# Row halves of the matrix array in a two-block network's recurrence: both heads of a pair side by side

## Chip, core and metric

The kernel runs on one core of one Trainium2 chip. The metric is the device time of one execution in microseconds (us); less is better. Five engines work beside each other: TensorE (PE in the profile, its weight loads PEld), VectorE (DVE), ScalarE (ACT), GpSimd (POOL), and SyncE (SP), which here issues nearly all transfers.

## What is computed

The reference runs two network blocks on a sequence of 1024 tokens. The first (windowed attention, a gated recurrence, a convolution and experts, two layers) is not touched by the change. The second block normalises its input, projects it with one wide matrix, and runs two branches: a gated unit that mixes blocks of 128 tokens (`gmlp`), and a recurrence with 16 heads of 64 channels:

```python
def wkv7_scan(r, w, k, v, kk, a):
    # S_t = S_{t-1} diag(w_t) + (S_{t-1} (-kk_t)) (kk_t * a_t)^T + v_t k_t^T ;  o_t = S_t r_t
    def step(state, inp):
        r_t, w_t, k_t, v_t, kk_t, a_t = inp
        sa = jnp.einsum('bhvk,bhk->bhv', state, -kk_t)
        state = (state * w_t[:, :, None, :]
                 + sa[..., None] * (kk_t * a_t)[:, :, None, :]
                 + v_t[..., None] * k_t[:, :, None, :])
        o_t = jnp.einsum('bhvk,bhk->bhv', state, r_t)
        return state, o_t
```

Both branches are then projected, gated, added and normalised. All of it is float32.

## The kernel before

The kernel doesn't step token by token. It cuts the sequence into 16 chunks of 64 tokens. Inside a chunk the dependence of each token on the earlier ones is a triangular 64x64 system for each head, which is inverted ahead of time; from chunk to chunk only the 64x64 state of each head is carried. Two heads make a pair: head p of a pair (p is 0 or 1) has its 64 channels on partitions 64p to 64p+63, and there are 8 pairs (q).

Four stages of the second block matter here.

- **Preparation of the pairs** (`rw_prepare`, `rw_pair`, lines 1525 to 1709). While TensorE computes the projection of r, k and v for pair q+1 (`gemm_feat`, whose matrix products are lines 168 to 170), the scaled vectors of pair q are formed. `s3` writes two tensors: `AR` (for each chunk alpha, the scaled -kk, and r) and `BK` (for each chunk beta and k; on the second head's rows in the other order, so that head p's beta lies at index p). `s4` forms the triangular matrices: beta times alpha for each head and chunk (line 1677), 16 products of which each reads all 128 partitions. For this the alphas lie in a tensor `raz` (`self.az`), set to zero once (line 1535), with head p's alphas copied to its own rows by ScalarE (line 1661); the zeros take the other head out of the sum. `s4` masks the result to `LT` and stores it.
- **Inverses** (`rw_inverses`, lines 1711 to 1764). The 64x64 triangular matrices are cut into 32x32 blocks. For four groups of pairs (b, two pairs each) the diagonal blocks are inverted by elementwise steps on GpSimd (the last group on VectorE), stored, and loaded again in another layout, and in four units of one pair and half a sequence the off-diagonal block follows by two products: `Lo` times the first block's inverse (line 1753) gives `Y`, and `Y` times the second block's inverse (line 1760) gives the block of `XT`, which is stored for the recurrence. Head p's blocks lie on partition quarters: the first product reads rows 64p to 64p+31 and writes partitions 64p+32 to 64p+63, the second the other way. Each head's 8 products are followed by its copy out of PSUM (`evac`, lines 123 and 125, in turn on ScalarE and VectorE).
- **The value path of the gated unit** (`gmlp_v`): a projection in 32 tiles.
- **The recurrence** (`rw_scan`, lines 1767 to 1897), in the background of the gated unit's and the gates' projections. For each chunk, two calls of `prepare` for the next chunk form all products of `BK` with `AR` of both heads (line 1796): each reads the 64 rows of one head, has 128 columns of weights and 128 columns of data. VectorE masks the result to `RL` and `MR`. The first call takes head 0, the second head 1; in each, two groups of four pairs, one PSUM bank after the other. The chunk's other products are lines 1836, 1849, 1870 and 1890; in line 1890 the second kind (`SV` with `AR`) uses 64x64 tiles, head p reading rows 64p and writing partitions 64p of one bank.

Background work is written as generators: after each tile of a projection, `tick` advances every generator of `self.bg` by one step (to its next `yield`). `drain` advances them with no projection between. A compiler pass orders each engine's instructions by this program order and by its own estimate of when they are ready, adds the semaphores, and gives each tile's memory free when its last user is done. All stages after the experts run on this one set of queues; each engine works through its queue in order.

```python
def tick(self):
    for _ in range(self.step):
        self.bg = [g for g in self.bg if next(g, self) is not self]
```

A float32 product is recorded as two matrix instructions, each with its weight load. The other names: `pt` are PSUM tiles of one bank (six in these stages), `pg` those of the projections (two).

Of the kernel before, what the change touches and what calls it, by code (L numbers as in the profile page):

```python
# [8 lines left out]
F32 = mybir.dt.float32  # L9
# [10 lines left out]
P = 128  # L20
# [1267 lines left out]
class Block2(Block1):  # L1288
# [236 lines left out]
    def rw_prepare(self, hi, lo, blocks, w, pool):  # L1525
        nc = self.nc
        t = lambda nm, n=512, b=1: pool.tile([P, n], F32, name=nm, tag=nm, bufs=b)
        m0 = t("rm0")
        nc.vector.memset(m0, 1.0)
        nc.vector.memset(m0.rearrange("p (c t) -> p c t", t=64)[:, :, 0:1], 0.0)  # L1530

        wa = pool.tile([P, 2, D], F32R, name="rwa")

        self.az = pool.tile([P, 2, 8, 64], F32, name="raz")
        nc.vector.memset(self.az, 0.0)
        cur = {}

        def mixed(f, t0, acc, out):

            pz, last = t("rpz", 513, 2), cur.get("p")  # L1540
            cur["p"] = pz
            if t0 == 0:
                nc.vector.memset(pz[:, 0:1], 0.0)  # L1543
            else:
                nc.vector.tensor_copy(pz[:, 0:1], last[:, 512:513])
            nc.scalar.copy(pz[:, 1:513], acc)
            if f % 4:
                nc.scalar.activation(out, acc, AF.Copy, scale=self.mu1[:, f:f + 1])
            else:
                nc.vector.tensor_scalar(out=out, in0=acc, scalar1=self.mu1[:, f:f + 1], scalar2=None, op0=ALU.mult)  # L1550
            nc.vector.scalar_tensor_tensor(out=out, in0=pz[:, 0:512], scalar=self.mu[:, f:f + 1], in1=out, op0=ALU.mult, op1=ALU.add)

        def ev_wa(c, t0, tn, acc):
            x = t("mz", 512, 2)
            mixed(0, t0, acc, x)
            self.act(x[0:64], x[0:64], AF.Tanh)
            for j in range(2):
                r, o = slice(64 * j, 64 * j + 64), slice(64 - 64 * j, 128 - 64 * j)
                nc.scalar.copy(wa[r, j, t0:t0 + tn], x[r])
                nc.vector.tensor_tensor(out=wa[o, j, t0:t0 + tn], in0=x[r], in1=f32(wa[r, j, t0:t0 + tn]), op=ALU.subtract)  # L1560

        self.d_Li = [self.tc.dram_tile([P, 32, 32], F32, name=f"dL{g}") for g in range(4)]
        self.d_Xi = [self.tc.dram_tile([P, 2, 32, 32], F32, name=f"dX{g}") for g in range(4)]

        def ev(c, t0, tn, acc):
            f = c // P
            q, kind = divmod(f - 1, 3)
            o = cur["rkv"[kind], t0] = t("m" + "rkv"[kind], 512, 4)
            mixed(f, t0, acc, o)

        def ev_z(c, t0, tn, acc):
            f = c // P
            z, sg = t("mz", 512, 2), t("mzs", 512, 1)
            mixed(f, t0, acc, z)
            self.act(sg, z, AF.Sigmoid)
            nc.gpsimd.tensor_tensor(out=z, in0=z, in1=sg, op=ALU.mult)
            nc.sync.dma_start(out=self.d_z[(f - 25) * P:(f - 24) * P, t0:t0 + tn], in_=z)

        self.gemm_feat(w, 0, P, hi, lo, blocks, ev_wa)
        inv = self.rw_inverses(t)  # L1580
        self.pairs = 0
        pair = iter(())
        for q in range(KT):
            self.bg = [pair, inv]
            self.gemm_feat(w, P + q * 384, 384, hi, lo, blocks, ev)
            for _ in pair:
                pass
            pair = self.rw_pair(q, dict(cur), wa, m0, pool)
        self.bg = [pair, inv]
        self.gemm_feat(w, 25 * P, D, hi, lo, blocks, ev_z)  # L1590

    def rw_pair(self, q, cur, wa, m0, pool):
        nc = self.nc
# [12 lines left out]
        for h in range(2):  # L1606
            e = d[h]
# [40 lines left out]
        def s3(h):  # L1648
            e = d[h]
            r, k, v, a, kk, sq, g, gp, ig, bv = (e[x] for x in ("r", "k", "v", "a", "kk", "sq", "g", "sg", "ig", "n"))  # L1650
            pb = self.pt()
            nc.tensor.matmul(pb, lhsT=self.bones, rhs=sq, start=True, stop=True)
            e["AR"], e["BK"] = AR, BK = t("AR", D), t("BK", D)
            ar = AR.rearrange("p (c x t) -> p c x t", x=2, t=64)
            bk = BK.rearrange("p (c x t) -> p c x t", x=2, t=64)
            V.scalar_tensor_tensor(out=ar[:, :, 0, :], in0=c3(kk), scalar=-1.0, in1=c3(gp), op0=ALU.mult, op1=ALU.mult)
            V.tensor_tensor(out=ar[:, :, 1, :], in0=c3(r), in1=c3(g), op=ALU.mult)
            V.tensor_tensor(out=a, in0=a, in1=kk, op=ALU.mult)
            for p in range(2):
                rows = slice(64 * p, 64 * p + 64)  # L1660
                nc.scalar.copy(self.az[rows, p], ar[rows, :, 0, :])
                V.tensor_tensor(out=bk[rows, :, p, :], in0=c3(a)[rows], in1=c3(ig)[rows], op=ALU.mult)
                V.tensor_tensor(out=bk[rows, :, 1 - p, :], in0=c3(k)[rows], in1=c3(ig)[rows], op=ALU.mult)
            V.tensor_tensor(out=bv, in0=pb, in1=v, op=ALU.mult)
            nc.sync.dma_start(out=self.d_bv[qs, 512 * h:512 * h + 512], in_=bv)
            for src, dst in ((AR, self.d_AR), (BK, self.d_BK)):
                nc.sync.dma_start(out=dst[8 * h:8 * h + 8, :, q, :].rearrange("c p x -> p c x"), in_=src.rearrange("p (c x) -> p c x", c=8))

        def s4(h):
            e = d[h]  # L1670
            bk = e["BK"].rearrange("p (c x t) -> p c x t", x=2, t=64)

            pl, pv = self.pt(), self.pt()
            LT, VT = t("LT"), t("VT")
            for c in range(8):
                for p in range(2):
                    nc.tensor.matmul(pl[64 * p:64 * p + 64, 64 * c:64 * c + 64], lhsT=bk[:, c, p, :], rhs=self.az[:, p, c, :], start=True,
                                     stop=True, skip_group_check=True)
            for i in range(4):
                nc.tensor.transpose(pv[:, P * i:P * i + P], e["v"][:, P * i:P * i + P], self.ident)  # L1680
            V.tensor_tensor(out=c3(LT), in0=c3(pl), in1=self.tri[:, 0, :].unsqueeze(1).to_broadcast([P, 8, 64]), op=ALU.mult)
# [29 lines left out]
    def rw_inverses(self, t):  # L1711
        nc = self.nc
        for b in range(4):
# [20 lines left out]
            for u in range(4):  # L1734
# [3 lines left out]
                for p in range(2):  # L1738
# [7 lines left out]
                    nc.sync.dma_start(out=X1[r1], in_=self.d_Xi[b][n0:n0 + 8, 0].rearrange("n s t -> s n t"))  # L1746
                    nc.sync.dma_start(out=Lo[r1], in_=self.d_LT[q, h, r1, :, 32:64])
                yield
                py = self.pt()
                for p in range(2):  # L1750
                    r1, r2 = slice(64 * p, 64 * p + 32), slice(64 * p + 32, 64 * p + 64)
                    for c in range(8):
                        nc.tensor.matmul(py[r2, 32 * c:32 * c + 32], lhsT=Lo[r1, c, :], rhs=X1[r1, c, :], start=True, stop=True,
                                         tile_position=(64 * p, 64 * p + 32), skip_group_check=True)
                    self.evac(Y[r2].rearrange("p c x -> p (c x)"), py[r2, :256])
                px = self.pt()
                for p in range(2):
                    r1, r2 = slice(64 * p, 64 * p + 32), slice(64 * p + 32, 64 * p + 64)
                    for c in range(8):
                        nc.tensor.matmul(px[r1, 32 * c:32 * c + 32], lhsT=Y[r2, c, :], rhs=XT[r2, c, 32:64], start=True, stop=True,  # L1760
                                         tile_position=(64 * p + 32, 64 * p), skip_group_check=True)
                    self.evac(XT[r1, :, 32:64], px[r1, :256].rearrange("p (c x) -> p c x", c=8))
                nc.sync.dma_start(out=self.d_XT[8 * h:8 * h + 8, :, q, :].rearrange("c p x -> p c x"), in_=XT)
                yield
# [2 lines left out]
    def rw_scan(self, pool):  # L1767
# [18 lines left out]
            nc.sync.dma_start(out=e["XT"], in_=self.d_XT[c])  # L1786
            return e

        def prepare(e, p):

            rows, oth = par[p]
            for g in groups:
                ps = self.pt()
                for q in range(g.start, g.stop):
                    x = (q - g.start) * P
                    nc.tensor.matmul(ps[:, x:x + P], lhsT=e["BK"][rows, q, :], rhs=e["AR"][rows, q, :], start=True, stop=True,  # L1796
                                     skip_group_check=True)
                pv = ps.rearrange("p (q x t) -> p q x t", q=4, x=2)
                V.tensor_tensor(out=e["RL"][p][oth, g, :], in0=pv[oth, :, 0, :], in1=self.tri[oth, 0, :].unsqueeze(1).to_broadcast([64, 4, 64]),
                                op=ALU.mult)  # L1800
# [15 lines left out]
        e = load(0)  # L1816
# [4 lines left out]
        for p in range(2):  # L1821
            rows, oth = par[p]
            V.memset(e["SV"][p][rows], 0.0)
            prepare(e, p)
            yield
        scale(e, 0)
        yield
# [1 line left out]
        for c in range(16):  # L1829
# [8 lines left out]
                for p in range(2):  # L1838
                    (nc.scalar.copy, V.tensor_copy)[p](R[p][par[p][0], g, :], pq(pr)[par[p][0]])
            if n:  # L1840
                prepare(n, 0)
            yield
            for g in groups:
                pu = self.pt()
# [9 lines left out]
            if n:  # L1854

                for p in range(2):
                    rows = par[p][0]
                    nc.gpsimd.tensor_tensor(out=n["SV"][p][rows], in0=e["SV"][p][rows],
                                            in1=self.gc[rows, :, c].unsqueeze(2).to_broadcast([64, KT, 64]), op=ALU.mult)
                prepare(n, 1)  # L1860
                scale(n, c + 1)
            yield
            if n:
# [192 lines left out]
```

## Time and profile before

| | before |
|---|---|
| runs | 4241.87, 4234.22, 4232.11 us (median 4234.22) |
| the profiled execution's own time | 4232.61 us |
| its span, first to last instruction | 4230.7 us |
| mean granted clock of TensorE | 0.961 |
| TensorE busy | 3844.5 us |
| VectorE, ScalarE, GpSimd busy | 2478.8, 1723.2, 1228.8 us |

The profile is of one execution. An engine's busy time is the time in which it had at least one instruction under way; matrix instructions are pipelined, so their own durations overlap and the distance between starts tells the pace. The clock is the share of full speed (2.4 GHz) that TensorE was granted; it has two levels, so 0.5 is 1.2 GHz and a value between is a mean over both. Start times count from the span's start. "x16" is the number of instructions that a row merges, and a bracket at the end of a row is the engine's idle time just before it and what ended it.

### The profile page before, as it was taken

The numbers are of one execution on the slowest core, as the hardware profiler recorded it, in microseconds if no ns is written. First come the engines' busy times: TensorE is split into PE (matmuls) and PEld (weight loads), VectorE is DVE, ScalarE is ACT, GpSimd is POOL, SyncE is SP. The second block draws the span as 40 slices with busy tenths as digits, with TensorE's granted clock in tenths as the row PEclk, the third lists the DMA queues.
The fourth block names the chain that finished last, engine by engine and source line by source line (L and its number), as shares of the span: only waits on it lengthen the run. The fifth ranks groups of instructions, "written<-read, shape, count | busy, mean of one in ns | idle before, by whom it ended". The sixth has DMA issues, their size and how long they took to land. (4 is left out here: it accounts for less than half of the span.)

```text
span 4230.7 us, 71359 instructions
## 1 busy us (share of the span) xinstructions
PE 3844.5 (91%) x28350; PEld 3103.0 (73%) x28350; DVE 2478.8 (59%) x4042; ACT 1723.2 (41%) x2900; POOL 1228.8 (29%) x1036
## 2 busy tenths in 40 slices
PE   7998889896999899888889599898899999999998
PEld 4877787764677688778777487676678888887777
DVE  3067745767677633785675798667776343222533
ACT  3134433622555432443462476554563211122522
POOL 2133233532232223322442222105451122211630
PEclk9999999998999999999999799999999999999999
DMA  7643222164899864332223899544545554444742
GB/s 257 198 123 112 83 70 83 55 217 175 275 305 305 285 209 136 112 97 73 80 91 120 285 367 371 179 126 118 140 126 148 139 135 123 134 136 126 246 129 90
DMA packets 543980, 695.71 MB, mean 164 GB/s; under 512 B 162592, under 2 KB 350368, under 8 KB 536992
## 3 DMA queue, kind: packets, MB, share of 16 engines
q1 hardware_dynamic: 531552, 653.40, 47.8%
q0 software_dynamic: 12096, 37.75, 3.6%
q8 instruction: 224, 3.67, 0.4%
q14 instruction: 108, 0.88, 0.1%
HBM read 530.61 MB, written 160.43 MB: 163 GB/s over the span
## 5 line engine op out<-in xcount | busy, mean ns | idle before, releaser
L154 DVE TENSOR_TENSOR wlo<-raw,whi 128x2048 fp32r<-128x2048 f32 (+2 forms) x320 | 594.6, 1868 | 374.2 <-ACT whi L151 364.2
L151 ACT CAST whi<-raw 128x2048 fp32r<-128x2048 f32 (+2 forms) x354 | 531.8, 1504 | 490.2 <-PE pg L169 200.7
L168 PE MATMUL pg<-hi,whi 128*128 128x512 f32 (+1 forms) x1808 | 719.3, 398 | 2.6 <-DVE cy L450 1.1
L170 PE MATMUL pg<-hi,wlo 128*128 128x512 f32 (+1 forms) x1808 | 698.6, 386 | 0.1
L169 PE MATMUL pg<-lo,whi 128*128 128x512 f32 (+1 forms) x1808 | 698.3, 386 | 0.0
L168 PEld LDWEIGHTS pg<-hi,whi 128*128 128x128 f32 x1808 | 345.9, 191 | 79.2 <-issue 7.1
L169 PEld LDWEIGHTS pg<-lo,whi 128*128 128x128 f32 x1808 | 345.8, 191 | 70.7 <-issue 7.1
L170 PEld LDWEIGHTS pg<-hi,wlo 128*128 128x128 f32 x1808 | 344.9, 191 | 68.0 <-DVE rpz L1543 0.5
L168 PE MATMUL pg<-whi,hi 128*128 128x256 f32 x1200 | 343.4, 286 | 2.2 <-ACT stg L379 2.2
L170 PE MATMUL pg<-whi,lo 128*128 128x256 f32 x1200 | 342.0, 285 | 0.0
L169 PE MATMUL pg<-wlo,hi 128*128 128x256 f32 x1200 | 341.5, 285 | 0.0
L168 PEld LDWEIGHTS pg<-whi,hi 128*128 128x128 f32 x1200 | 229.9, 192 | 13.5 <-issue 5.7
L169 PEld LDWEIGHTS pg<-wlo,hi 128*128 128x128 f32 x1200 | 230.2, 192 | 7.8 <-issue 5.9
L170 PEld LDWEIGHTS pg<-whi,lo 128*128 128x128 f32 x1200 | 229.9, 192 | 7.3 <-issue 6.1
L154 POOL TENSOR_TENSOR wlo<-raw,whi 128x1024 fp32r<-128x1024 f32 (+1 forms) x34 | 97.6, 2874 | 434.9 <-ACT whi L151 434.8
L168 PE MATMUL pg<-whi,xh 128*128 128x512 f32 x512 | 209.6, 409 | 0.0
L169 PE MATMUL pg<-wlo,xh 128*128 128x512 f32 x512 | 204.9, 400 | 1.9 <-DVE wlo L154 1.8
L170 PE MATMUL pg<-whi,xl 128*128 128x512 f32 x512 | 204.6, 400 | 0.8 <-DVE xl L1038 0.8
L1102 POOL DMA_INDIRECT x<-eo,iT x32 | 99.1, 3096 | 249.0 <-DVE eo L1094 235.5
L379 ACT COPY stg<-pg 128x256 f32<-128x256 f32 x118 | 43.8, 371 | 237.8 <-PE pg L170 211.7
L502 PE MATMUL pt<-hZQ,hKS 128*64 128x64 f32 x2592 | 98.0, 229 | 45.8 <-DVE hKS L538 28.6
L1030 POOL DMA_INDIRECT xg<-xn,iT x32 | 56.7, 1772 | 284.8 <-PE pt L1139 267.7
(459 smaller groups left out, 8362.8 us busy)
## 6 DMA issues: line engine op xcount, KB each, us to landing
raw<-in_w_exp_gate_dram SPq DMA_DIRECT2D x64, 1024.0 KB
raw<-in_w_exp_up_dram SPq DMA_DIRECT2D x64, 1024.0 KB
raw<-in_w_exp_down_dram SPq DMA_DIRECT2D x64, 1024.0 KB
raw<-in_k_win_dram SPq DMA_DIRECT2D x124, 512.0 KB
wm<-in_w_mod_dram SPq DMA_DIRECT2D x36, 1024.0 KB
AR<-AR SPq DMA_DIRECT2D x32, 512.0 KB
BK<-BK SPq DMA_DIRECT2D x32, 512.0 KB
mxr<-mix SPq DMA_DIRECT2D x18, 512.0 KB
```

The costliest lines, as they stand in the source:

```text
L151: nc.scalar.copy(hi, r)
L154: i = eng.tensor_tensor(out=lo, in0=r, in1=f32(hi), op=ALU.subtract)
L168: mm(out, lhsT=lh, rhs=rh, start=start, stop=False)
L169: mm(out, lhsT=lh, rhs=rl, start=False, stop=False)
L170: mm(out, lhsT=ll, rhs=rh, start=False, stop=stop)
L379: nc.scalar.copy(s, acc)
L502: nc.tensor.matmul(ps[64 * (c % 2):64 * (c % 2) + 64, c // 2 * 64:c // 2 * 64 + 64], lhsT=KS[:, cc * 64:(cc + 1) * 64], rhs=zq[:, c * 64:( ...
L1030: nc.gpsimd.indirect_dma_start(out=g, out_offset=None, in_=d_h[:, :], in_offset=bass.IndirectOffsetOnAxis(ap=iT[:, e:e + 1], axis=0))
L1102: nc.gpsimd.indirect_dma_start(out=d_x[:, :], out_offset=bass.IndirectOffsetOnAxis(ap=iT[:, e:e + 1], axis=0), in_=o, in_offset=None, comp ...
```

## The change

Three things are changed in the second block, and one `yield` is added.

1. `s4` reads the alphas from `AR` directly: each head's product contracts over its own 64 rows and writes its own 64 partitions. The tensor `raz`, its zeroing and the 32 copies to it are gone.
2. In the inverses, the two heads' products alternate in one group, for the first as for the second product; the copies follow after both heads. Between the copies to `Y` and the second product stands a `yield`, so a unit takes three steps and not two.
3. `prepare` takes a group of four pairs, not a head. It has two PSUM banks, one for each head, and alternates between the heads; the first call takes pairs 0 to 3, the second pairs 4 to 7.

```diff
-        self.az = pool.tile([P, 2, 8, 64], F32, name="raz")
-        nc.vector.memset(self.az, 0.0)
...
-                nc.scalar.copy(self.az[rows, p], ar[rows, :, 0, :])
...
             for c in range(8):
                 for p in range(2):
-                    nc.tensor.matmul(pl[64 * p:64 * p + 64, 64 * c:64 * c + 64], lhsT=bk[:, c, p, :], rhs=self.az[:, p, c, :], start=True,
-                                     stop=True, skip_group_check=True)
+                    rows = slice(64 * p, 64 * p + 64)
+                    nc.tensor.matmul(pl[rows, 64 * c:64 * c + 64], lhsT=bk[rows, c, p, :], rhs=ar[rows, c, 0, :], start=True, stop=True,
+                                     skip_group_check=True)
...
+                halves = [(slice(64 * p, 64 * p + 32), slice(64 * p + 32, 64 * p + 64)) for p in range(2)]
                 py = self.pt()
-                for p in range(2):
-                    r1, r2 = slice(64 * p, 64 * p + 32), slice(64 * p + 32, 64 * p + 64)
-                    for c in range(8):
+                for c in range(8):
+                    for p, (r1, r2) in enumerate(halves):
                         nc.tensor.matmul(py[r2, 32 * c:32 * c + 32], lhsT=Lo[r1, c, :], rhs=X1[r1, c, :], start=True, stop=True,
                                          tile_position=(64 * p, 64 * p + 32), skip_group_check=True)
+                for r1, r2 in halves:
                     self.evac(Y[r2].rearrange("p c x -> p (c x)"), py[r2, :256])
+                yield
                 px = self.pt()
-                for p in range(2):
-                    r1, r2 = slice(64 * p, 64 * p + 32), slice(64 * p + 32, 64 * p + 64)
-                    for c in range(8):
+                for c in range(8):
+                    for p, (r1, r2) in enumerate(halves):
                         nc.tensor.matmul(px[r1, 32 * c:32 * c + 32], lhsT=Y[r2, c, :], rhs=XT[r2, c, 32:64], start=True, stop=True,
                                          tile_position=(64 * p + 32, 64 * p), skip_group_check=True)
+                for r1, r2 in halves:
                     self.evac(XT[r1, :, 32:64], px[r1, :256].rearrange("p (c x) -> p c x", c=8))
...
-        def prepare(e, p):
+        def prepare(e, g):
-            rows, oth = par[p]
-            for g in groups:
-                ps = self.pt()
-                for q in range(g.start, g.stop):
-                    x = (q - g.start) * P
+            pss = [self.pt() for p in range(2)]
+            for q in range(g.start, g.stop):
+                x = (q - g.start) * P
+                for p, ps in enumerate(pss):
+                    rows = par[p][0]
                     nc.tensor.matmul(ps[:, x:x + P], lhsT=e["BK"][rows, q, :], rhs=e["AR"][rows, q, :], start=True, stop=True,
                                      skip_group_check=True)
+            for p, ps in enumerate(pss):
+                oth = par[p][1]
                 pv = ps.rearrange("p (q x t) -> p q x t", q=4, x=2)
...
-            prepare(e, p)
+            prepare(e, groups[p])
...
-                prepare(n, 0)
+                prepare(n, groups[0])
...
-                prepare(n, 1)
+                prepare(n, groups[1])
```

## Rows read from the trace of the kernel before

**Rows 1.** The page's first part: busy us (share of the span) and instructions.

```profile
PE 3844.5 (91%) x28350; PEld 3103.0 (73%) x28350; DVE 2478.8 (59%) x4042; ACT 1723.2 (41%) x2900; POOL 1228.8 (29%) x1036
```

**Rows 2.** Busy time by stretch: us, engines' busy us (instructions), granted clock, DMA share, GB/s.

```profile
2760.00:2920.00 160.00, 150.21 (x792) 116.70 (x790) 117.91 (x174) 89.69 (x155) 55.91 (x69) 0.98 0.38 112
2920.00:3130.00 210.00, 189.15 (x1306) 142.61 (x1307) 157.93 (x233) 99.47 (x180) 101.71 (x132) 0.91 0.50 135
3130.00:3345.00 215.00, 210.16 (x1804) 183.54 (x1803) 112.31 (x245) 95.29 (x182) 23.45 (x16) 1.00 0.49 137
3365.00:3897.00 532.00, 529.47 (x4669) 441.23 (x4670) 180.89 (x334) 108.45 (x202) 121.13 (x85) 1.00 0.46 128
```

**Rows 3.** Single lines on TensorE: instructions, ns min/median/max, first to last start us, form.

```profile
L1796 PE MATMUL pt<-AR,BK x512: 272/272/373, 3364.8 to 3873.5; 64*128 64x128 f32 x171
...
L1753 PE MATMUL pt<-X,Lo x512: 191/191/257, 2925.2 to 3308.3; 32*32 32x32 f32 x171
...
L1760 PE MATMUL pt<-XT,Y x512: 184/191/257, 2928.4 to 3313.3; 32*32 32x32 f32 x171
```

**Rows 4.** Timeline of TensorE, a call of `prepare`: start us, us, what.

```profile
3364.83 2.05 PE L1796 MATMUL pt<-AR,BK 64*128 64x128 f32 x16
3366.81 0.38 PE L1507 MATMUL pt<-gws,gV 128*128 128x128 f32 x1
```

**Rows 5.** Timeline of TensorE, output of a chunk, line 1890.

```profile
3405.94 0.68 PE L1890 MATMUL pt<-AR,SV 64*64 64x64 f32 x16
3406.55 0.69 PE L1890 MATMUL pt<-MR,UV 128*64 128x64 f32 x16
```

**Rows 6.** Timeline of TensorE, line 1677 and what follows it.

```profile
2788.70 1.15 PE L1677 MATMUL pt<-raz,BK 128*64 128x64 f32 x32
2789.78 0.66 PE L1680 MATMUL pt<-k_ident,mv 128*128 128x128 f32 x4
```

**Rows 7.** Timeline of TensorE, one group of the inverses' first product.

```profile
2968.99 0.69 PE L1753 MATMUL pt<-X,Lo 32*32 32x32 f32 x16
2969.61 0.50 PE L169 MATMUL pg<-lo,whi 128*128 128x512 f32 x1
```

**Rows 8.** Timeline of TensorE, where head 1's first product meets head 0's second.

```profile
3205.68 0.59 PE L1753 MATMUL pt<-X,Lo 32*32 32x32 f32 x13
3206.09 0.21 PE L1760 MATMUL pt<-XT,Y 32*32 32x32 f32 x1
...
3206.20 0.57 PE L1760 MATMUL pt<-XT,Y 32*32 32x32 f32 x13
3206.70 0.50 PE L169 MATMUL pg<-lo,whi 128*128 128x512 f32 x1
```

**Rows 9.** TensorE's waits from 2760 to 3365 us: total us, times, longest.

```profile
PE pt L1652 <- DVE rsq L1641: 13.1, 2, 7.9
PE pt L1760 <- issue: 10.3, 4, 4.4
...
PE pt L1760 <- ACT XT L123: 2.1, 2, 1.2
```

**Rows 10.** Timeline of TensorE around one of these waits.

```profile
3119.30 0.91 PE L1677 MATMUL pt<-raz,BK 128*64 128x64 f32 x22
3122.72 0.97 PE L1760 MATMUL pt<-XT,Y 32*32 32x32 f32 x16 [2.51 <-issue]
```

**Rows 11.** Timeline of VectorE at the same place.

```profile
3122.19 0.43 DVE L125 COPY Y<-pt 32x256 f32<-32x256 f32 x1
```

**Rows 12.** Copies to `raz`: instructions, ns min/median/max, first to last start.

```profile
L1661 ACT COPY raz<-AR x32: 603/620/625, 2783.4 to 3174.7; 64x512 f32<-64x512 f32 x32
```

**Rows 13.** The squares of `gmlp_v`, one for each of its 32 tiles.

```profile
L1449 DVE CUSTOM_DVE_ANT_0 mzs<-mz x32: 418/426/1952, 3250.2 to 3346.0; 128x256 f32<-128x256 f32 x32
```

**Rows 14.** Timeline of SP: the load of `gws`.

```profile
3350.21 0.50 SPq L1471 DMA_DIRECT2D gws<-in_k_gws_dram  x1
```

**Rows 15.** Timeline of TensorE: the products that need `gws`.

```profile
3356.28 1.98 PE L1481 MATMUL pt<-gws,gs 128*128 128x512 f32 x4 [2.86 <-DVE gws L1473]
```

More of the change, by code (lines that the diff above doesn't have):

```diff
@@ L1670, in s4 @@
             e = d[h]
-            bk = e["BK"].rearrange("p (c x t) -> p c x t", x=2, t=64)
+            ar, bk = (e[x].rearrange("p (c x t) -> p c x t", x=2, t=64) for x in ("AR", "BK"))
             pl, pv = self.pt(), self.pt()
```

## The prediction

> **What bounds the kernel now.** I read the page's first part for the engines, then the stretches of the last block, then the lines that the diff touches, then TensorE's waits. TensorE is busy 91% of the span, more than any other engine [rows 1]. In the recurrence stretch, 3365 to 3897 us, it is busy 529.5 of 532 us at full clock; VectorE is busy 181 us there, ScalarE 108. What is taken from TensorE there comes off the end. The preparation before it falls into three parts [rows 2]. From 3130 to 3345 us TensorE is again nearly full (210 of 215). From 2920 to 3130 us it is busy 189 of 210 us, VectorE 158, and the mean granted clock is 0.91: no engine is full, TensorE waits for results and then runs slowly. A saving there is worth less than its size.
>
> **What was profiled.** The span is 4230.7 us and the execution's time 4232.6 us, 1.9 us around it. The median of the runs is 4234.2, 1.6 us higher. All sums start from 4232.6.
>
> **The products of a chunk (`prepare`).** Line 1796 has 512 matrix instructions [rows 3]. Each float32 product is recorded as two, and a call makes 16 of them, so there are 32 calls. One call takes from 3364.83 to 3366.81, 1.98 us [rows 4]: 0.12 us for each instruction, all 16 on the same half of the array's rows. The change makes the same 32 calls with the same 16 instructions, but neighbours lie on opposite halves and write different banks. The trace has no 64x128 tiles that alternate between row halves. The nearest rows are 32x32 products of lines 1753 and 1760 where one group runs into the next, on other rows, other columns and another bank [rows 8]. Thirteen alone take 0.41 us, 0.032 each; six alternating singly (the row at 3206.09 and the five left out behind it) take 0.11 us to 3206.20, 0.018 each. So tiles that share neither rows nor columns run side by side at 0.57 of the price. For `prepare` the bounds are no gain (both halves share one path for their weights) and half. A group's fixed part follows from two groups of 64-column tiles: 32 instructions take 1.08 us [rows 6], 16 take 0.61 us [rows 5], so one costs 0.029 and the fixed part is 0.14. A new call is then 0.14 + 8 x (1.98 - 0.14)/16 = 1.06 us, and 32 calls save 32 x 0.92 = 29 us. I take this end, because the alternating rows of [rows 8] come close to a half. The VectorE work behind a call (four products with the mask) is the same in count; it now comes together at the end of a call, while TensorE goes on with the projection. VectorE's 181 of 532 us hide it [rows 2].
>
> **The inverse blocks' products.** Lines 1753 and 1760 have 512 instructions each [rows 3], 64 groups of 16. A group at full clock lasts 2968.99 to 2969.61, 0.62 us [rows 7], of which 16 x 0.032 = 0.50 is work and 0.12 is fixed. Now both heads make one group of 32 alternating instructions: 32 x 0.018 + 0.12 = 0.70 us against 1.24. That is 0.54 us for each of 32 pairs, 17 us of TensorE (bounds: 0, and 20 if the price falls to a half). The trace has 36 of the 64 groups after 3130 us, where TensorE is full, so 9.7 us count there. Of the other 7.6 I count half, 3.8, since TensorE has idle time in that part.
>
> The Trainium skill speaks against this part. Its page "TensorEngine Tiling (Array Packing)", section "Restrictions and Gotchas", says that different row tiles can't access the same PSUM bank at the same time; both heads' products here go to one bank. The trace disagrees where it can be tested: in line 1890 the 64x64 tiles of both row halves write one bank, and their 16 instructions take 3405.94 to 3406.55, 0.61 us, exactly like tiles of all 128 rows in the L1677 group by the fixed part worked out above [rows 5, 6]. By the rule the 17 us would be nothing; by the row they stand.
>
> **The wait between the two products.** Before, the second product stands right behind the first's copy to `Y` in the same step, and TensorE waits: 10.3 us in four places and 2.1 us in two [rows 9]. The view gives "issue" for the four. The one at 3122.72 shows what it was: the copy of `Y` on VectorE started at 3122.19 and took 0.43 us, after other work of that queue [rows 10, 11]. The new `yield` puts a whole projection tile between copy and second product, so these 12.4 us go. I credit 9.6: the 2.6 us after 3130 us in full, and 7 of 9.8 us before, where TensorE may meet the next VectorE result. The waits also lower the clock: from 2920 to 3130 us a mean of 0.91 over 210 us is 19 us of full clock lost [rows 2]. These waits are about 40% of the idle time there, the rest belonging mostly to L1652's 13.1 us [rows 9]; I credit half of that share, 4 us.
>
> **The moved steps.** An inverse group of four units needs 8 + 4 x 2 = 16 steps before and 8 + 4 x 3 = 20 after; the first starts at step 18 of 96 (48 projection tiles of r, k and v, 16 of z, 32 of `gmlp_v`). Groups follow one another, so the last second product moves from step 81 to step 97, one after the last tile of `gmlp_v`. In the trace these products end at 3313 us and `gmlp_v` at 3346 us [rows 3, 13]. What moves with them: the loads of `XT`, `X1` and `Lo` and the store of `XT` on SP's queue, the copies on ScalarE and VectorE. Two places can pay. First, after `gmlp_v` SP loads `gws` at 3350.21 and TensorE already waits 2.86 us for it [rows 14, 15]; the last `XT` store now stands ahead of that load and waits for its copy. `gmlp_v`'s own statistics end at about the same time, so I take 1 us (bounds 0 and 8). The scan's own load of `XT` comes later still. Second, the transfers of the second inverse group now meet another step of a pair; the 7.9 us wait of L1652 is what such a meeting costs at worst [rows 9]. I take 3 us (bounds 0 and 8).
>
> **What is removed or costs nothing.** The 32 copies to `raz`, 0.62 us each [rows 12], leave ScalarE, which is busy 99 of 210 us [rows 2]; I count nothing (up to 3 us of gain through earlier copies). Line 1677's products go from 128-row tiles with zeros to 64x64 tiles on the diagonal. That is the form of line 1890, at the same price [rows 5, 6]: nothing.
>
> **Sum.** 29 + 9.7 + 3.8 + 9.6 + 4 = 56.1 saved, 4 lost, and 1 for loads of the scan that now come a little late: 51 us. 4232.6 - 51 = 4181 us.
>
> **Rivals.**
> A. The row halves share one path for weights, so `prepare` gains nothing: 4181 + 29 = 4210. For it: the alternating rows differ in columns too [rows 8]. Against it: nothing in them hints at a shared path. Chance 0.10.
> B. Two row tiles of one bank take turns in the inverse blocks: 13.5 us less, 4195. This is the time by the Tiling page's rule. Against it stands line 1890 [rows 5]. Chance 0.05.
> C. From 2920 to 3130 us VectorE is the limit and the transfers collide: the 3.8, 7 and 4 us fall away and 5 more are lost, 4201. For it: VectorE's 158 of 210 us [rows 2]. Against it: most of these waits end with one small copy [rows 11]. Chance 0.08.
> D. Slower: each change of row half inside a `prepare` call makes the array empty itself, at the group's fixed 0.14 us. With 512 changes that is 72 us in place of a gain of 29: 4181 + 29 + 72 = 4282. It decides from 22/512 = 0.043 us a change. Against it: neighbours in [rows 8] start 0.01 to 0.03 us apart. The Tiling page's section "Key Properties" has a drain only for a change of mode, not of tile, which the trace's rows bear out. Chance 0.04.
>
> **How the numbers follow.** The forecast has 0.73. Its own range is 4160 to 4200: all bounds in favour (29 + 20 + 12.4 + 8 + 3) give 4160; half of the 14.8 us from 2920 to 3130 gone, and both meeting places at their full 8 us (7 and 5 more), give 4200. To hold 8 in 10 the range takes in B, most of C and half of A: 4160 to 4210. A change within 0.2% (8.5 us) is about what the measurement can't tell from none. A to C are all faster than that. Faster 0.93, same 0.03 (A with C), slower 0.04 (D).
>
> **What would show it.** A `prepare` call of about 1.06 us in the timeline; inverse groups of 32 in about 0.70 us; L1677 still near 1.08; no wait of the second product for `Y`; last inverse product just behind `gmlp_v`; the recurrence stretch about 29 us shorter with TensorE still full. I am wrong if a call stays near 2 us, or if TensorE's waits elsewhere in 2920 to 3130 us grow by what was saved.

## The result, and the profile after

| | before | after |
|---|---|---|
| median of the runs, us | 4234.06 | 4192.65 |
| lowest and highest | 4232.11, 4241.87 | 4187.87, 4195.25 |
| ratio, 95% interval | | 0.990 [0.9888, 0.9913] |
| profiled execution: time, span | 4232.61, 4230.7 | 4195.25, 4193.5 |

The change saves 41.4 us, 1.0%. The forecast was 4181, in a range of 4160 to 4210. Right in direction and range, it promised some 10 us too much.

The two profiles can't be compared by their spans. These are the first transposes of the second block, before and after (instructions, ns min/median/max, first to last start):

```profile
L279 PE MATMUL pt<-dg,x x128: 275/275/582, 2700.5 to 2718.9; 128*128 128x128 f32 x128
```

```profile
L279 PE MATMUL pt<-dg,x x128: 274/275/580, 2710.8 to 2728.8; 128*128 128x128 f32 x128
```

Everything ahead of them is unchanged, and it took 10.3 us longer in the profile after. Over the profiles below this start lies anywhere from 2694.9 to 2710.8 us. So I compare stretches that are cut at the program's own marks: T0, the first L279; T1, the last square of `gmlp_v`; T2, the first product of `prepare`; T3, the last product of the recurrence with `SV`. The marks after, by line:

```profile
L1449 DVE CUSTOM_DVE_ANT_0 mzs<-mz x32: 418/426/1056, 3238.5 to 3334.9; 128x256 f32<-128x256 f32 x32
```

```profile
L1797 PE MATMUL pt<-AR,BK x512: 271/272/374, 3361.0 to 3838.1; 64*128 64x128 f32 x171
```

```profile
L1893 PE MATMUL pt<-AR,SV x512: 217/219/268, 3399.0 to 3866.4; 64*64 64x64 f32 x171
```

Before, T1 and T2 are 3346.0 and 3364.8 [rows 13, 3], and T3 is 3901.9. In us:

| stretch | before | after | difference | forecast |
|---|---|---|---|---|
| T0 to T1, preparation and `gmlp_v` | 645.5 | 624.1 | -21.4 | -24 |
| T1 to T2, the turn to the recurrence | 18.9 | 26.0 | +7.1 | +1 |
| T2 to T3, the recurrence | 537.0 | 505.5 | -31.5 | -28 |
| T3 to the end | 328.9 | 327.0 | -1.9 | 0 |
| T0 to the end | 1530.2 | 1482.6 | -47.6 | -51 |

**The recurrence.** A call of `prepare` after, against 1.98 us in [rows 4] (TensorE's timeline: start us, us, what):

```profile
3360.95 1.16 PE L1797 MATMUL pt<-AR,BK 64*128 64x128 f32 x16
3362.04 1.16 PE L1507 MATMUL pt<-gws,gV 128*128 128x128 f32 x8
```

From start to next start it is 1.09 us; 1.06 were forecast. 32 calls save 28.5 us, and TensorE is still full (stretches: us, engines' busy us in the order of [rows 2], clock):

```profile
3365.00:3862.00 497.00, 496.43 (x4632) 409.18 (x4630) 173.32 (x328) 108.69 (x203) 119.35 (x83) 1.00 0.47 134
```

**The inverses' products.** Against two groups of 0.62 us [rows 7], one of 32:

```profile
2962.05 0.69 PE L1751 MATMUL pt<-X,Lo 32*32 32x32 f32 x32
2962.67 0.50 PE L168 MATMUL pg<-hi,whi 128*128 128x512 f32 x1
```

It takes 0.62 us, as long as half its instructions did. The 32 of a line-1674 group (1677 before) lie on 64x64 tiles now and still take 1.08 us, as in [rows 6]:

```profile
2798.66 1.15 PE L1674 MATMUL pt<-AR,BK 64*64 64x64 f32 x32
2799.74 0.66 PE L1677 MATMUL pt<-k_ident,mv 128*128 128x128 f32 x4
```

**TensorE's waits.** After, from 2760 to 3365 us (total us, times, longest), to be held against [rows 9]:

```profile
PE pt L1759 <- DMA XT<-dX: 11.6, 3, 5.6
PE pt L1649 <- DVE rsq L1638: 9.3, 1, 9.3
PE pt L1634 <- DVE rpz L1542: 6.5, 3, 3.1
PE pt L1674 <- DVE BK L1658: 4.4, 3, 2.7
```

The second product (L1759) hardly waits for `Y` any more (0.3 us). It waits for `XT`'s loads, almost as long in all: 11.6 us against 12.4, of which 5.6 come behind T1. And the sum of TensorE's idle time from T0 to T1 hardly moved; here are the stretches before and after:

```profile
2701.00:3346.00 645.00, 608.68 (x4212) 494.15 (x4212) 420.83 (x714) 315.78 (x577) 183.69 (x220) 0.96 0.44 124
```

```profile
2711.00:3335.00 624.00, 588.69 (x4176) 480.69 (x4176) 422.23 (x709) 290.12 (x541) 189.83 (x220) 0.96 0.45 128
```

Idle is 645.0 - 608.7 = 36.3 us before and 624.0 - 588.7 = 35.3 after. So nearly all of the 21 us of this stretch is busy time, 20.0 us less: the product groups are shorter, and more of them stay whole than with the alternation alone (see the runs on the yield below). The granted clock is 0.96 in both.

**Where the new waits come from.** At the end of `gmlp_v`, on SP's queue and on TensorE after:

```profile
3334.02 0.39 SPq L1763 DMA_DIRECT2D XT<-XT  x1
...
3336.78 1.80 SPq L1740 DMA_DIRECT2D XT<-dX  x4
```

```profile
3340.57 1.35 PE L1759 MATMUL pt<-XT,Y 32*32 32x32 f32 x32 [5.55 <-DMA XT<-dX]
3342.83 0.80 PE L168 MATMUL pg<-hi,whi 128*128 128x512 f32 x1 [0.91 <-DVE XT L125]
```

`XT` has one buffer. The last unit's loads can be issued only after the store of the unit before, and they land 4 us later. With the steps moved behind `gmlp_v`, no projection tile is left to work on meanwhile. The last product then stands at the head of TensorE's queue, and the next projection behind it starts at half clock. The turn to the recurrence in one row, before and after:

```profile
3346.00:3365.00 19.00, 16.14 (x71) 12.35 (x70) 11.55 (x26) 6.42 (x8) 2.68 (x2) 1.00 0.89 254
```

```profile
3335.00:3361.00 26.00, 19.50 (x106) 15.30 (x104) 12.05 (x29) 7.11 (x10) 1.76 (x2) 0.80 0.95 261
```

Of the 7 us, 3.6 are more idle time (6.5 against 2.9), and TensorE is busy 3.4 us longer, at a mean granted clock of 0.80, not 1.00.

At the start of z, SP after:

```profile
3119.95 0.58 SPq L141 DMA_DIRECT2D raw<-in_k_win_dram  x1
3135.15 0.34 SPq L1574 DMA_DIRECT2D rz<-mz  x1
3135.60 1.88 SPq L1740 DMA_DIRECT2D XT<-dX  x4
```

and SP's wait and TensorE's:

```profile
SPq L1574 <- POOL mz L1573: 14.5, 1, 14.5
```

```profile
3138.24 0.28 PE L1759 MATMUL pt<-XT,Y 32*32 32x32 f32 x2 [5.38 <-DMA XT<-dX]
```

The first store of z waits for its product on GpSimd, which stands behind the whole elementwise inversion of the third group. The chain of work that ended last runs along that inversion (L1722 and L1725 in turn) to its end and on to z's store:

```profile
3131.15 2.31 POOL Xi L1728
3133.45 1.68 POOL mz L1573
3135.15 2.00 DMA rz<-mz
```

The moved unit's loads of `XT` stand behind that store.

### The profile page after: what moved, and what is told of

It reads as the page before. It is cut to its first block, busy times and chain, and to the rows that moved or that the text cites. A ratio compares the mean times of both kernels' runs of the same rounds, so it can differ in the third digit from the quotient of the medians.

```text
span 4193.5 us, 71296 instructions
## 1 busy us (share of the span) xinstructions
PE 3802.6 (91%) x28350; PEld 3067.9 (73%) x28350; DVE 2473.1 (59%) x4041; ACT 1696.5 (40%) x2865; POOL 1237.3 (30%) x1036
## 5 line engine op out<-in xcount | busy, mean ns | idle before, releaser
L170 PE MATMUL pg<-hi,wlo 128*128 128x512 f32 (+1 forms) x1808 | 697.9, 386 | 0.1
L169 PE MATMUL pg<-lo,whi 128*128 128x512 f32 (+1 forms) x1808 | 697.3, 386 | 0.0
L169 PEld LDWEIGHTS pg<-lo,whi 128*128 128x128 f32 x1808 | 346.4, 192 | 70.0 <-issue 6.5
L170 PEld LDWEIGHTS pg<-hi,wlo 128*128 128x128 f32 x1808 | 345.2, 191 | 67.9 <-DVE wlo L154 0.6
L169 PE MATMUL pg<-wlo,hi 128*128 128x256 f32 x1200 | 343.9, 287 | 2.1 <-DVE wlo L154 2.1
L170 PE MATMUL pg<-whi,lo 128*128 128x256 f32 x1200 | 343.6, 286 | 0.0
L169 PEld LDWEIGHTS pg<-wlo,hi 128*128 128x128 f32 x1200 | 231.8, 193 | 10.9 <-issue 5.9
L170 PEld LDWEIGHTS pg<-whi,lo 128*128 128x128 f32 x1200 | 231.8, 193 | 7.1 <-issue 6.1
L169 PE MATMUL pg<-wlo,xh 128*128 128x512 f32 x512 | 204.9, 400 | 2.5 <-DVE wlo L154 2.5
L170 PE MATMUL pg<-whi,xl 128*128 128x512 f32 x512 | 204.8, 400 | 0.8 <-DVE xl L1038 0.8
```

Source lines behind the costliest of these rows:

```text
L169: mm(out, lhsT=lh, rhs=rl, start=False, stop=False)
L170: mm(out, lhsT=ll, rhs=rh, start=False, stop=stop)
```

## The experiments

Each was timed against the kernel before on the same chip; "call" is the time of a call of `prepare` in us. The last columns come from the run's profile.

| run | median, us | before | ratio [95%] | T0-T1 | T1-T2 | T2-T3 | call |
|---|---|---|---|---|---|---|---|
| before | | | | 645.5 | 18.9 | 537.0 | 1.98 |
| the change | 4192.65 | 4234.06 | 0.990 [0.9888, 0.9913] | 624.1 | 26.0 | 505.5 | 1.09 |
| prepare alone | 4201.20 | 4229.47 | 0.994 [0.9926, 0.9954] | 644.0 | 19.2 | 506.2 | 1.09 |
| alternation alone | 4216.47 | 4229.47 | 0.997 [0.9959, 0.9981] | 633.0 | 19.2 | 533.8 | 1.98 |
| yield alone | 4227.12 | 4229.47 | 0.9994 [0.9986, 1.0003] | 640.1 | 26.4 | 532.7 | 1.98 |
| no zeros alone | 4226.10 | 4229.47 | 0.999 [0.9981, 1.0] | 643.3 | 20.6 | 533.4 | 1.98 |
| change without the yield | 4187.51 | 4229.42 | 0.9905 [0.989, 0.992] | 631.9 | 20.6 | 506.4 | 1.09 |
| heads in turn | 4205.73 | 4229.42 | 0.9945 [0.9924, 0.9965] | 622.9 | 27.3 | 522.8 | 1.64 |
| loads ahead | 4184.51 | 4229.42 | 0.989 [0.9872, 0.9908] | 624.7 | 21.5 | 505.8 | 1.09 |
| yield in two groups | 4183.41 | 4229.42 | 0.9888 [0.987, 0.9905] | 625.3 | 21.9 | 505.3 | 1.09 |
| the change again | 4191.07 | 4231.94 | 0.9902 [0.9885, 0.9918] | 624.7 | 26.0 | 505.6 | 1.09 |
| without the yield again | 4185.94 | 4231.94 | 0.9885 [0.9868, 0.9901] | 633.6 | 21.8 | 505.2 | 1.09 |
| yield in two groups again | 4186.75 | 4231.94 | 0.9891 [0.9874, 0.9907] | 625.9 | 20.4 | 505.3 | 1.09 |
| two buffers for rn | 4187.75 | 4231.94 | 0.9894 [0.9877, 0.991] | 628.6 | 22.4 | 505.9 | 1.09 |

**The four parts, each alone on the kernel before.** The edits are those of the diff above, one at a time.

Part 3, `prepare`:

> Only the third part of the change: prepare alternates between the heads, all else as before. The prediction's reading (neighbouring row halves run side by side): calls of about 1.09 us in place of 1.98, 29 us less, 4234 to 4205. Rival A (the halves share one path for weights): calls near 1.98 us and no change of time. The trace of the changed kernel already shows 1.09 us a call; this run shows what that is worth alone, and whether the time outside the recurrence stays as it was.

28.3 us less, the prediction's 29. The recurrence alone is 30.8 us shorter, the rest as it was. Rival A is out.

Part 2 without its yield:

```diff
                 for r1, r2 in halves:
                     self.evac(Y[r2].rearrange("p c x -> p (c x)"), py[r2, :256])
-                yield
                 px = self.pt()
```

> Only the alternation of the inverse blocks' products, without the new yield. The prediction's reading: a group of 32 in about 0.62 to 0.70 us in place of two of 0.62, 13.5 us less, 4220; the second product still waits for the copy of Y, now for both heads' copies, so that wait stays at 12 us or grows. Rival: with no head-1 product left between head 0's copy and head 0's second product, the wait grows by what the alternation saves, and the time stays within 8 us of 4234.

13.0 us less, as the sum had it (9.7 + 3.8). The wait for `Y` stays: 10.7 us in four places from 2760 to 3365 us. TensorE's busy time in the preparation falls by 14.5 us, not by 20, and its idle time grows by 2.5 (to be held against the 645.00 row above):

```profile
2700.00:3333.00 633.00, 594.18 (x4213) 478.67 (x4213) 423.15 (x714) 313.74 (x576) 182.86 (x220) 0.96 0.44 127
```

The reason is in the runs without the yield below: 24 of the 32 groups are issued in two pieces.

The yield alone:

```diff
                     self.evac(Y[r2].rearrange("p c x -> p (c x)"), py[r2, :256])
+                yield
                 px = self.pt()
```

> Only the new yield, the products in the old order of heads. The prediction's reading: 9.6 us of waits and 4 us of low clock go, 4 us are lost at the moved steps: 4224. Rival (the yield costs as much as it gives): the waits for Y go, but the second product meets late loads of XT where the moved units lie behind the z stores and at the end of gmlp_v, some 10 to 15 us with the low clock behind them: 4230 to 4237.

2.4 us less, an interval that holds no change. The preparation is 5.4 us shorter, with 31.1 us of idle time in place of 36.3, and the turn to the recurrence 7.5 us longer. So of the 13.6 us of waits and low clock about 5 came, and the moved steps cost 7.5, not 4. The rival's sum fits, its account only in part: from 2760 to 3365 us TensorE waits 0.4 us for loads of `XT`, and not at all for them at the start of z.

Part 1, without zeros:

> Only the first part: 64x64 tiles in s4, no raz, no copies to it. The prediction's reading: no change, 4231 to 4234 (ScalarE has room for the 20 us of copies). Rival: the copies to raz held up the projections' copies on ScalarE, and 5 us or more go, 4229 or less.

3.4 us less, at the edge of what can be told from nothing; neither theory is decided.

The four medians add up to -47.1 us, against the -41.4 of all four together. The difference is within the runs' spread.

**Which part of `prepare` does it.** The changed kernel, with the two loops exchanged:

```diff
-            for q in range(g.start, g.stop):
-                x = (q - g.start) * P
-                for p, ps in enumerate(pss):
-                    rows = par[p][0]
+            for p, ps in enumerate(pss):
+                rows = par[p][0]
+                for q in range(g.start, g.stop):
+                    x = (q - g.start) * P
```

> The changed kernel with prepare's products in the order of heads: first head 0's four into one bank, then head 1's four into the other; same instructions, banks and copies. If it is the alternation of row halves that halves a call (the prediction), a call goes back to about 1.98 us and the time rises by about 28 us. Rival: the two banks or the copies at the end make the difference, and a call stays near 1.1 us.

Neither. A call takes 1.64 us (TensorE's timeline of this run):

```profile
3369.14 1.71 PE L1797 MATMUL pt<-AR,BK 64*128 64x128 f32 x16
3370.78 0.50 PE L168 MATMUL pg<-hi,whi 128*128 128x512 f32 x1
```

That is 0.34 us less than 1.98. At 0.115 us an instruction [rows 4, worked out in the prediction] it is three of them: where the first half's run ends and the second's begins, three of each run side by side, as in [rows 8], where three of L1753 and three of L1760 alternate. So runs on different halves do overlap, but here only over about three instructions of each, and alternation one by one makes all 16 overlap. What sets the three no run shows. The change of bank alone does nothing: the old call also wrote one bank in its first eight instructions and another in the next eight, on one half, and took 1.98 us [rows 4]. The calls cost 32 x (1.64 - 1.09) = 17.6 us, and the recurrence is 17.3 us longer.

**The yield.** The changed kernel without it, twice:

> The changed kernel without the new yield. The prediction's reading (the yield is worth about 9.6 us): the second product waits for the copy of Y again, 10 us or more in TensorE's waits, and the time is about 9 us above the changed kernel's, some 4197 by a before of 4230. Rival (the yield costs at the end of gmlp_v and behind the z stores what it gives): within 4 us of the changed kernel, 4185 to 4190, with the wait for Y back and the 5 us waits for loads of XT gone.

> The changed kernel without the new yield, again. The prediction's reading: about 9 us above the changed kernel. Rival, which the first run favours (the yield costs as much as it gives): within 3 us of it on either side.

The wait for `Y` is back (13.6 us in six places in the first run, 12.4 in five in the second), and here it has its name:

```profile
2985.45 1.06 PE L1758 MATMUL pt<-XT,Y 32*32 32x32 f32 x30 [4.39 <-DVE Y L125]
```

The preparation is 8 to 9 us longer than with the yield, the turn 4 to 5 us shorter. Waits are the smaller part of the 8: TensorE idles 36.5 and 38.9 us in the preparation without the yield, 35.3 and (in the repeat) 36.2 with it. The larger part is busy time, 595.5 us in the first run against 588.7:

```profile
2695.00:3327.00 632.00, 595.50 (x4212) 480.06 (x4213) 422.47 (x713) 294.12 (x545) 181.66 (x220) 0.96 0.45 127
```

Without the yield most groups are issued in two pieces, two instructions ahead and 30 later, with projection products between:

```profile
3190.75 0.39 PE L169 MATMUL pg<-lo,whi 128*128 128x512 f32 x1
3190.98 0.39 PE L170 MATMUL pg<-hi,wlo 128*128 128x512 f32 x1
3191.30 0.24 PE L1758 MATMUL pt<-XT,Y 32*32 32x32 f32 x2
3191.47 0.50 PE L168 MATMUL pg<-hi,whi 128*128 128x512 f32 x1
3191.81 0.40 PE L169 MATMUL pg<-lo,whi 128*128 128x512 f32 x1
...
3194.06 0.69 PE L1758 MATMUL pt<-XT,Y 32*32 32x32 f32 x30 [1.39 <-DVE Y L125]
3194.67 0.76 PE L169 MATMUL pg<-lo,whi 128*128 128x512 f32 x1
```

From L170's start to that of L169 behind the piece it is 0.83 us. Two projection products take 2 x 0.23 = 0.46 without it, so the small piece costs 0.37 us, and the 30 still take 0.61. Counted in the timelines, 24 of the 32 groups are in pieces without the yield, 17 with the yield in two inverse groups (the run below) and 11 with it in all four. 13 pieces fewer at 0.37 us and a last group of 0.62 that the yield moves behind T1 make 5.4 of the 6.8 us. Why the compiler pass takes two instructions ahead is not shown.

By the medians the kernel is no slower without the yield: 0.9885 and 0.9905 against 0.990 and 0.9902, the intervals overlapping. By the profiles from T0 to the end it is 3 to 8 us slower (1485.4 and 1490.5 against 1482.6 and 1483.1). Neither is clear, and the rival, that the yield costs about what it gives, holds.

**Without the moved end.** The yield in the first two inverse groups alone, twice, so that the last product comes at step 89 of 96:

```diff
-                yield
+                if b < 2:
+                    yield
                 px = self.pt()
```

> The changed kernel with the new yield in the first two of the four inverse groups alone, so that the last product comes at step 89 of 96. If the end of gmlp_v costs about 6 us, that goes and the time is 4 to 7 us below the changed kernel's. Rival: the copies of Y in the last groups are waited for instead, and nothing is won.

> The yield in the first two inverse groups alone, again. If the end of gmlp_v costs the changed kernel about 6 us, this one is 4 to 7 us below the changed kernel in this batch; if what is saved there comes back as other waits, within 3 us.

The turn is 4 to 6 us shorter, the preparation within 2 us of that with the yield. In the batch that holds both, the median is 4.3 us below the changed kernel's, with overlapping intervals: it agrees with the first theory and doesn't prove it by time.

**The loads.** Two buffers for `XT`, `X1` and `Lo`, and each unit's loads issued beside the first product of the unit before:

```diff
+            nxt = fetch(0)
+            yield
             for u in range(4):
...
+                if u < 3:
+                    nxt = fetch(u + 1)
                 py = self.pt()
```

> The changed kernel, the inverse units' XT, X1 and Lo with two buffers, and each unit's loads issued one unit ahead, beside the first product of the unit before: two steps a unit, with the yield kept. If the 5.6 us wait at the end of gmlp_v and the 5.4 us wait at the start of z come from loads that stand behind the store of the unit before or behind z's stores, both go, the last inverse product ends well before gmlp_v does, and the time falls by 6 to 12 us below the changed kernel's, 4176 to 4182 by a before of 4230. Rival: the waits come from the transfers' own duration or the queue's length, and the time stays within 3 us of the changed kernel's.

Both waits for `XT` are gone and the turn is 4.5 us shorter, but the wait next in line grew (TensorE's waits, 2760 to 3365 us):

```profile
PE pt L1649 <- DVE rsq L1638: 26.0, 4, 11.4
```

It was 9.3 after the change. By the ratios this version is some 4 us below the changed kernel, not the 6 to 12 expected, and the intervals overlap. It doesn't tell late loads from late steps either: with two steps a unit, its last inverse product starts 31 us ahead of T1, not 7 us behind it.

**The wait that is in every profile.** L1649's 9.3 us (L1652's 7.9 before) come from `rn`: its next writer on VectorE waits for the store to `rbv`, and that stands on SP behind the store of `Xi`, which waits for GpSimd. Two buffers for `rn`, on top of the yield in two groups:

```diff
-            n = e["n"] = t("rn")
+            n = e["n"] = t("rn", 512, 2)
```

> The yield in the first two inverse groups alone, and two buffers for rn, the tile from which the store to rbv is taken. In every profile so far TensorE waits 8 to 9.5 us for rsq, because rn's next writer on VectorE waits for that store, and the store stands on SP's queue behind the store of Xi, which waits for GpSimd. If that is the cause, this wait goes and the time falls by 6 to 12 us below the run beside it with one buffer. Rival: TensorE meets the next result that is late, as with the other waits, and the time stays within 4 us.

The wait for rsq is gone, and in its place TensorE's timeline has this:

```profile
2929.99 0.28 PE L1751 MATMUL pt<-X,Lo 32*32 32x32 f32 x2 [12.82 <-issue]
```

The inverse unit's own first product is the next in the queue, and it starts no earlier: 226.0 us behind T0, against 224.0 with one buffer. What it waits for the view doesn't name. No time is won; the rival holds.

**The changed kernel again.**

> The changed kernel once more, beside the three versions below on the same chip, because they lie within 10 us of each other. Its profile has two stretches to repeat: the part ahead of the second block, in which nothing was changed and which was 10 us longer in the first profile of the changed kernel (if that is chance, it is within 5 us of the kernel before here), and the 5.5 us waits for XT at the start of z and at the end of gmlp_v (if they are the program's order, they are there again).

The waits are there again, and T1 to T2 is 26.0 again: they belong to the program's order. (For the second the view names ScalarE's `gst`; the loads of `XT` stand in the same place on SP.)

```profile
3136.54 0.28 PE L1759 MATMUL pt<-XT,Y 32*32 32x32 f32 x2 [5.28 <-DMA XT<-dX]
...
3338.73 1.39 PE L1759 MATMUL pt<-XT,Y 32*32 32x32 f32 x32 [5.36 <-ACT gst L109]
```

The start of the second block was 2708.6 us, 8 above the kernel before: by the 5 us that was expected, that isn't chance. In the other profiles it was 2694.9 to 2709.3, with the same kernel (the one without the yield) at 2694.9 and 2704.3. I read its 10 us as scatter, but that is not shown: there is no second profile of the kernel before.

## Why the prediction was right, and where it was too high

1. **`prepare`**: right by its own step. 1.06 us a call was forecast, 1.09 measured; -29 us was forecast, -28.3 measured alone. The choice of the upper bound, from a row with other tiles, was borne out. About 3 of the 31.5 us in the recurrence stretch aren't the call's: the three runs that leave the recurrence alone and change only what lies ahead have 3 to 4 us less there too. I don't know why.
2. **The inverses' products**: the group is 0.62 us, not 0.70, and in the whole change TensorE's busy time falls by 20 us, where 17 were forecast. Alone, the 13.5 us that were counted were found as 13.0, but that is luck: half of the saving was struck off where TensorE has idle time, while in the run TensorE's busy time fell by 14.5 us and not by 20, with most groups in two pieces, and its idle time grew by 2.5. Rival B does not act here: both heads write one bank, and the group takes the time of one head's. The prediction's own test of it went in a circle, since the fixed part by which line 1890 was judged had been worked out from that line; line 1674 is the better one, 1.08 us with both row halves in one bank as with 128 rows.
3. **The wait for `Y`**: the wait went, as forecast, but the credit of 9.6 + 4 us was the step that failed. Idle time from T0 to T1 fell by 1 us, and by 5.2 with the yield alone. Several chains of results are late here by a few us, and TensorE works through its queue in order: the next product that isn't ready takes over the wait. The prediction said so of VectorE's results and allowed 2.8 us for it; it should have allowed most. What the yield did give in the changed kernel, groups that stay whole, stands in no term of the sum.
4. **The moved steps**: the place at the end of `gmlp_v` was named, and mis-sized: 7.1 us, not 1, of a bound of 8. It was costed by the store that stands ahead of `gws`. What TensorE waits for is the load of the last unit behind the store of the unit before, with one buffer, and no work is left to cover it; half clock follows. With the last product ahead of the end of `gmlp_v` the turn is 4 to 6 us shorter. The other place cost a wait of 5.4 us and 3 were allowed, but for another reason: not transfers that collide, but z's store ahead on SP, waiting for GpSimd. With the yield alone this wait is not there.
5. **No zeros**: nothing forecast, 3.4 us measured alone, at the edge of the interval. TensorE's price is unchanged, as forecast.

Rival C came true in part, with 4201 as its price: the waits paid little. That VectorE is the limit there, as it has it, no run shows. Rivals A, B and D are refuted by the durations above.

## What to carry to other kernels

A small matrix product can be halved in price when its neighbour in the queue lies on other rows of the array, as `prepare` shows. Look first whether its data columns set its pace. Here they don't: products of 128 weight columns start 0.11 us apart with 128 data columns [rows 4, by the prediction's working], and as far apart with 256 (TensorE's timeline after):

```profile
3330.07 0.28 PE L169 MATMUL pg<-wlo,hi 128*128 128x256 f32 x1
3330.18 0.28 PE L170 MATMUL pg<-whi,lo 128*128 128x256 f32 x1
```

Check that the products are neighbours one by one, not half a group apart, and that their groups stay whole in the timeline. Take TensorE's shorter groups at full value where it is full, but a wait that goes from an in-order queue only counts when the next thing in that queue is ready; add up the idle time of the whole stretch before crediting any single wait. When a step is moved, look at what it now stands behind on the transfer queue, and at what is still there to cover the last one.

## What was not expected of the hardware

Here TensorE overlapped runs on different row halves only over about three instructions: two runs of eight give 1.64 us where strict alternation gives 1.09 and one half alone 1.98. And 32 alternating 32x32 instructions that write one bank on separate partitions take the 0.62 us of 16. A piece of two such instructions between projection products costs 0.37 us, and the other 30 are no shorter for it.
